# Three edits behind the attention of an encoder layer: which engine forms the differences, when one matrix is split, and how many buffers the embeddings use

## The chip, the cores and the metric

The kernel runs on one core of a Trainium2 chip. Its engines work through queues of their own, each in order: TensorE (PE; its weight loads are listed as PEld), VectorE (DVE), ScalarE (ACT), GpSimd (POOL) and SyncE (SP), which issues the DMAs here. The metric is the device time of one execution in microseconds.

## The reference

One layer of a bidirectional encoder is applied to two sequences of 2048 tokens and width 1024 that share the weights, all in float32. Cut to what matters:

```
proj = rms_norm(x) @ w_in                    # 3328 columns
o_a  = windowed_attention(...) * silu(g_a)   # 8 heads, window +-128
o_b  = neighbourhood_attention(...) * silu(g_b)
x    = x + concat([o_a, o_b]) @ w_out        # 1024 x 1024
gate = sigmoid(x @ w_ple_gate)               # 1024 x 1024
y    = x + (p @ w_ple) * gate                # p: 2048 x 256
```

The change lies in the last three lines: the product with `w_ple` (the embeddings) and the two square products, called the tail here.

## The kernel before

**Precision.** Each matmul of two float32 operands is done as three matmuls of rounded operands. An operand is split: ScalarE writes its rounded copy (hi), VectorE subtracts that from the original (lo), and TensorE adds hi·hi, hi·lo and lo·hi in one PSUM bank. Weights are split by `split_w` (L163 on ACT, L164 on DVE), the tail's activations by `piece` (L1064 on ACT, L1065 on DVE).

**Stream and attention.** Until about 1874 us a generator gives out projection matmuls one by one, and the attention's steps are placed between them at set shares of a unit's cost. `pump` takes one waiting weight split from the list `jobs`; `flush` takes all up to a given one. The last five units of the attention have no projections left, so `ple_ahead(0)` to `ple_ahead(4)` fill them: the embeddings of 512 tokens each, eight output tiles `m` of six matmuls. A result goes from PSUM (`pple`, tag "pj", three banks) by an ACT copy (L870) into a buffer `ev`, and from there by a DMA (L871) into the array `ple_d`. In this part `ev` has two buffers. The tag "sq", also with two buffers of that size, belongs to the projections: the squares and, last, the values `vb` (L692), which a DMA stores (L700).

**Behind the attention** `ple_ahead(5)` to `ple_ahead(7)` run with `tail=True`. They use five buffers of the tag "s". Each output tile also calls `pump` (L865). The list is empty there, but for one case: the last loop is halted after 24 matmuls, the first four operands of the tail are made, and `load_q(0, "s2")` issues four loads of 256 KB and puts their splits on the list. The rest of the loop then takes these four splits between its result copies. The loads for "s1", "s3" and "s4" follow when the loop is done.

**The tail** computes each square product for 1024 tokens by Strassen's scheme (Winograd's form): seven block products in place of eight, at the price of sums of blocks. The sums of weight blocks (s1 to s4) were formed earlier and lie in `sums`. The sums of activation blocks are `combos`: per group 16 subtractions of 128x512 tiles (L1028), four on DVE and twelve on POOL. There are eight groups, four of stage 0 (`w_out`) and four of stage 1 (`w_ple_gate`). A group has seven steps `i`; step `i` runs `product(m, mi)` for four `mi`, 12 matmuls each (L1082). In step `i` the loop calls, for each `mi`: `combos` (in steps 0, 2 and 3), two `piece`s of the next step's operand (for `mi` 0 and 1), then the product and its `result`. In steps 0, 2, 3 and 6 a result starts (stage 0: a DVE sum L1117; stage 1: an ACT copy L1120, in step 6 a tanh from PSUM); in steps 1, 4 and 5 it is finished with a DVE sum (L1126). A finished result of stage 1 goes through tanh on ACT (L1130) and two DVE instructions (L1131, L1132). Eight accumulators share PSUM; the ones of step 1 use the three banks of the tag "sc" for four products, and steps 2, 3 and 6 add to the banks that step 0 began.

**Order.** `P` is `tc.keep_in_program_order`: what it wraps stays in the order of the program on its engine. All of the tail is wrapped, and TensorE's order is fixed throughout. In the splits of the next stage, `load_q(1, ...)` in group 3, four splits are flushed behind each of the steps 3 to 6 of group 3 and 0 to 2 of group 4.

The call that takes the four splits of "s2" if they are still waiting, ahead of step 1 of group 0:

```
if n == 0:
    flush({1: "0s2", 2: "0s1", 3: "0s3", 5: "0s4"}.get(i))
```

Of the kernel before, what the change touches and what calls it, by code (L numbers as in the profile page):

```python
# [11 lines left out]
F32 = mybir.dt.float32  # L12
# [68 lines left out]
TW = 512  # L81
# [17 lines left out]
def emit(ctx, tc, io):  # L99
    nc = tc.nc  # L100
# [4 lines left out]
    def ptile(shape, tag, name):  # L105
        tag = PSM.get(tag, tag)
        return pp.tile(shape, F32, tag=tag, name=name, bufs=PSB[tag])
# [61 lines left out]
    def pump(n=1):  # L169
        for _, job in jobs[:n]:  # L170
            job()
        del jobs[:n]

    def flush(key):
        pump(max((i + 1 for i, (k, _) in enumerate(jobs) if k == key), default=0))
# [35 lines left out]
    def mm(out, lhsT, rhs, start, stop):  # L211
        pinned(nc.tensor.matmul(out, lhsT, rhs, start=start, stop=stop))  # L212
# [61 lines left out]
    ap = ab_stack.enter_context(tc.tile_pool(name="ab", bufs=1))  # L274
# [534 lines left out]
    def load_p(n):  # L809
        if n < len(tiles):  # L810
            s, u = tiles[n]
            p_st[n] = []
            for k in range(2):
                st = main.tile([128, TW], F32, tag="stage", name="p32", bufs=2)
                nc.sync.dma_start(st, io["p_t"][s][128 * k:128 * k + 128, TW * u:TW * u + TW])
                p_st[n].append(st)

    def split_p(n, later=False):

        t = p_rs[n] = main.tile([128, 2, 2, TW], F32R, tag="xr", name="p_r", bufs=2)  # L820

        def job(hi, lo, src):
            nc.scalar.copy(hi, src)
            nc.vector.tensor_tensor(out=lo, in0=src, in1=hi.bitcast(F32), op=ALU.subtract)
        for k, src in enumerate(p_st.pop(n)):
            todo = partial(job, t[:, k, 0], t[:, k, 1], src)
            if later:
                jobs.append((f"p{n}", todo))
            else:
                todo()  # L830
# [19 lines left out]
    def ple_ahead(n, tail=False):  # L850

        load_p(n + 1)
        for m in range(KT):
            ps = ptile([128, TW], "pj", "pple")
            if m == 5 and n + 1 < len(tiles):
                split_p(n + 1)
            flush("p")
            flush("p0")
            for k in range(2):
                w, c = early["p"][2 * (m // 4) + k], 128 * (m % 4)  # L860
                for i, (a, b) in enumerate(((0, 0), (0, 1), (1, 0))):
                    mm(ps, w[:, a, c:c + 128], p_rs[n][:, k, b], k == 0 and i == 0, k == 1 and i == 2)
                    yield 215
            if n > 0 or m > 5:
                pump()  # L865
            if tail:
                ev = main.tile([128, TW], F32, tag="s", name="ev", bufs=SB)
            else:
                ev = ap.tile([128, TW], F32, tag="ev", name="ev", bufs=2)
            P(nc.scalar.copy(ev, ps))  # L870
            nc.sync.dma_start(ple_d[n][:, m], ev)  # L871

# [40 lines left out]
    def paired(f, n):  # L913
# [19 lines left out]
        else:  # L933
            for name in ("a11", "a12", "a22"):
                load_early(name)
        w_b[half] = w

    stream = chain(*(paired(f, last[f]) if f in last else filler(f) for f in range(2, 6 * NT) if f - 1 not in last),
                   *(ple_ahead(n) for n in range(AHEAD)))
    drain(stream, 24)  # L940
    done = 2
# [32 lines left out]
    with tc.tile_pool(name="c", bufs=1, reuse_waits="tile") as op:  # L974
# [44 lines left out]
        def each(fn, k, *blocks):  # L1019

            views = [t[:, k] for t, _ in blocks]
            if any(by_col for _, by_col in blocks):
                views = [v.rearrange("p (c r x) -> p r c x", c=4, x=16) if by_col else
                         v.rearrange("p (r c x) -> p r c x", c=4, x=16) for v, (_, by_col) in zip(views, blocks)]
            P(fn(*views))

        def less(eng, n, k, out, a, b):
            each(lambda x, y, z: eng.tensor_tensor(out=x, in0=y, in1=z, op=ALU.subtract), k,  # L1028
                 *(raws[n, i] for i in (out, a, b)))

        def combos(n, i, k):

            if i == 0:
                if k == 0:
                    raws[n, 4] = op.tile([128, 4, TW], F32, tag="raw", name="raw", bufs=5), False
                less(nc.vector, n, k, 0, 2, 0)
                less(nc.gpsimd, n, k, 4, 3, 0)
            elif i == 2:
                less(nc.gpsimd, n, k, 2, 3, 2)
            elif i == 3:  # L1040
                less(nc.gpsimd, n, k, 4, 1, 4)

        pair = []

# [92 lines left out]

        load_raw(0, 0)
        drain(ple_ahead(AHEAD, True))
        load_raw(0, 1)  # L1140
        drain(ple_ahead(AHEAD + 1, True))
        flush("a22")
        for _ in range(4):
# [13 lines left out]
        for m in range(7 * len(groups)):  # L1157
            n, i = divmod(m, 7)
            if i >= 3:
                load_raw(n + 1, i - 3)  # L1160
            if n == 0:
                flush({1: "0s2", 2: "0s1", 3: "0s3", 5: "0s4"}.get(i))
            for mi in range(4):
                combos(n, i, mi)
                for k in range(2 * mi, 2 * mi + 2) if mi < 2 else ():
                    piece(m + 1, k)
                result(n, i, mi, product(m, mi))
            if n == n_o - 1:
                load_q(1, STEPS[i])
                if i >= 3:  # L1170
                    flush("1" + STEPS[i - 3])
            elif n == n_o and i < 3:
                flush("1" + STEPS[i + 4])
# [76 lines left out]
```

## Time and profile before

| | us |
|---|---|
| median of 3 runs | 2554.75 (2552.64 to 2556.46) |
| the profiled execution, its own time | 2549.44 |
| its span, first to last instruction | 2547.2 |
| TensorE busy | 2486.1 (98%) |
| VectorE busy | 1946.9 (76%) |
| ScalarE busy | 1443.8 (57%) |
| GpSimd busy | 733.2 (29%) |

The profile page is one execution. Its parts used here are the busy times, the chain of work that ended last, the waits (who waited for whom, total us, times, longest), the groups by line (busy, mean ns, idle before), the timeline (start, duration, engine, line, what; in brackets the idle time before it and its releaser) and a table by stretches of time. TensorE's mean granted clock is 0.994 of full speed.

### The profile page before, as it was taken

What the parts mean: (1) busy time and instruction counts of PE and PEld (TensorE: products, weight loads), DVE (VectorE), ACT (ScalarE), POOL (GpSimd) and SP (SyncE); (2) the same over time, 40 slices, a digit from 0 to 9 for tenths busy, and PEclk for the clock granted to TensorE, in tenths of its full rate; (3) what the DMA queues carried; (4) which work ended last, traced back from release to release, by engine and by line L of the source; (5) the groups of instructions that cost most, each with busy time, mean ns of one, the idle gap of its engine ahead of it and who ended that gap; (6) DMA issues with size and microseconds to landing.
All of it is one profiled execution on the core that took longest, in us unless ns stands there. A gap on an engine that the chain in (4) does not pass through costs nothing.

```text
span 2547.2 us, 41396 instructions
## 1 busy us (share of the span) xinstructions
PE 2486.1 (98%) x12912; PEld 2091.2 (82%) x12912; DVE 1946.9 (76%) x5764; ACT 1443.8 (57%) x3469; POOL 733.2 (29%) x969
## 2 busy tenths in 40 slices
PE   8999999999989999999899999999989999999998
PEld 7888888888877888888788888887777888878787
DVE  7888888888887777787877877877635655677876
ACT  6666666666664566666666666666753222344343
POOL 3333323332322333333233332222102221132320
PEclk9999999999999999999999999999999999999999
DMA  5323332111143555555755555456776455746664
GB/s 198 103 97 110 104 97 93 53 59 57 63 112 113 167 185 158 183 182 161 238 164 165 184 176 156 145 156 213 250 253 213 158 166 180 269 159 213 222 231 158
DMA packets 236044, 405.40 MB, mean 159 GB/s; under 512 B 30864, under 2 KB 85264, under 8 KB 230416
## 3 DMA queue, kind: packets, MB, share of 16 engines
q1 hardware_dynamic: 235824, 402.75, 49.5%
q8 instruction: 103, 1.69, 0.3%
q14 instruction: 117, 0.96, 0.1%
HBM read 297.79 MB, written 122.70 MB: 165 GB/s over the span
## 4 chain that ended last, share of the span: by engine, by line
PE 83%; DVE 8%; DMA 3%; ACT 3%; issue 2%; POOL 0%; SPq 0%; ACTq 0%; DVEq 0%; POOLq 0%
PE pqk L212 13%; PE pvg L212 13%; PE acca L1082 11%; PE accc L1082 8%; PE pq L212 6%; PE pg L212 6%; PE scb L212 3%; PE ptb L215 3%; PE pk L212 3%; PE pob L212 3%; PE sc L212 3%; PE po L212 3%; PE pt L215 3%; PE pple L212 2%; DMA ple_d<-ev 1%
## 5 line engine op out<-in xcount | busy, mean ns | idle before, releaser
L243 ACT ACTIVATE s<-s,nm 128x384 f32<-128x384 f32 (+4 forms) x512 | 307.2, 601 | 337.9 <-DVE nm L238 209.8
L212 PE MATMUL pvg<-wb,xr 128*128 128x512 f32 x1536 | 462.1, 408 | 0.0
L212 PE MATMUL pqk<-wa,xr 128*128 128x512 f32 x1536 | 443.9, 411 | 0.0
L308 POOL TENSOR_TENSOR xr<-stx,xr 128x512 fp32r<-128x512 f32 x190 | 244.7, 1295 | 187.3 <-ACT xr L307 181.2
L212 PEld LDWEIGHTS pqk<-wa,xr 128*128 128x128 f32 x1536 | 267.0, 189 | 37.8
L212 PEld LDWEIGHTS pvg<-wb,xr 128*128 128x128 f32 x1536 | 268.4, 190 | 31.6
L1028 POOL TENSOR_TENSOR raw<-raw 128x512 f32<-128x512 f32 x96 | 152.3, 1614 | 460.7 <-DVE raw L1028 284.8
L1064 ACT CAST opd<-raw 128x512 fp32r<-128x512 f32 x224 | 130.4, 620 | 256.6 <-PE acca L1082 105.5
L1065 DVE TENSOR_TENSOR opd<-raw,opd 128x512 fp32r<-128x512 f32 x224 | 183.1, 853 | 120.0 <-ACT opd L1064 120.0
L212 PE MATMUL pg<-wb,xr 128*128 128x512 f32 x768 | 232.1, 410 | 0.0
L212 PE MATMUL pq<-wa,xr 128*128 128x512 f32 x768 | 219.8, 399 | 2.0 <-DVE wa L160 1.6
L798 POOL TENSOR_TENSOR o_tb<-otb 128x256 f32<-128x256 f32 x64 | 47.9, 748 | 549.9 <-DVE otb L791 466.4
L1082 PE MATMUL accc<-opd,wb 128*128 128x512 f32 x768 | 178.6, 392 | 2.8 <-DVE r L1126 2.8
L1082 PE MATMUL acca<-opd,s 128*128 128x512 f32 x768 | 177.5, 390 | 2.8 <-ACT r L1120 2.4
L1082 PE MATMUL acca<-opd,wa 128*128 128x512 f32 x768 | 175.9, 389 | 0.5 <-DVE opd L1065 0.5
L1082 PEld LDWEIGHTS accc<-opd,wb 128*128 128x128 f32 x768 | 145.2, 189 | 33.5 <-DVE r L1126 3.2
L1082 PEld LDWEIGHTS acca<-opd,s 128*128 128x128 f32 x768 | 143.5, 188 | 35.5 <-ACT r L1120 4.0
L1082 PEld LDWEIGHTS acca<-opd,wa 128*128 128x128 f32 x768 | 144.1, 188 | 30.8 <-DVE opd L1065 0.9
L212 PEld LDWEIGHTS pq<-wa,xr 128*128 128x128 f32 x768 | 139.1, 188 | 25.2 <-DVE wa L160 3.0
L212 PEld LDWEIGHTS pob<-p_t,vw 128*128 128x128 f32 (+2 forms) x832 | 132.5, 189 | 31.4 <-DVE p_t L772 7.1
L212 PEld LDWEIGHTS pg<-wb,xr 128*128 128x128 f32 x768 | 138.0, 190 | 20.6
L227 DVE CUSTOM_DVE_ANT_0 s<-scb,bias 128x288 f32<-128x288 f32 (+3 forms) x256 | 141.2, 552 | 16.8 <-PE scb L212 13.8
(171 smaller groups left out, 5330.8 us busy)
## 6 DMA issues: line engine op xcount, KB each, us to landing
stx<-x_b SPq DMA_DIRECT2D x128, 256.0 KB
vw<-v_d SPq DMA_DIRECT2D x112, 256.0 KB
stx<-x_a SPq DMA_DIRECT2D x64, 256.0 KB
stn<-x_n SPq DMA_DIRECT2D x64, 256.0 KB
v_d<-vb SPq DMA_DIRECT2D x64, 256.0 KB
ple_d<-ev SPq DMA_DIRECT2D x64, 256.0 KB
xres<-x_r SPq DMA_DIRECT2D x64, 256.0 KB
x_d<-r SPq DMA_DIRECT2D x64, 256.0 KB
```

The costliest lines, as they stand in the source:

```text
L212: pinned(nc.tensor.matmul(out, lhsT, rhs, start=start, stop=stop))
L215: pinned(nc.tensor.transpose(out, in_, eye))
L227: nc.vector.tensor_tensor_reduce(out=s[:, :n], in0=ps[:, :n], in1=bias, scale=1.0, scalar=-3.0e38, op0=ALU.add, op1=ALU.max, accum_out=sm[ ...
L243: ex = nc.scalar.activation(ss[i][:, :n], ss[i][:, :n], AF.Exp, bias=nm[:, i:i + 1], accum_out=den[:, i:i + 1])
L308: low.tensor_tensor(out=lo, in0=raw, in1=hi.bitcast(F32), op=ALU.subtract)
L798: nc.gpsimd.tensor_tensor(out=o_t, in0=got["ot"][:, :, 0], in1=got["ot"][:, :, 1], op=ALU.add)
L1028: each(lambda x, y, z: eng.tensor_tensor(out=x, in0=y, in1=z, op=ALU.subtract), k, *(raws[n, i] for i in (out, a, b)))
L1064: P(nc.scalar.copy(hi, v))
L1065: P(nc.vector.tensor_tensor(out=lo, in0=v, in1=hi.bitcast(F32), op=ALU.subtract))
L1082: pinned(nc.tensor.matmul(ps, w[k][:, a, c:c + 128], o[:, b], start=i in (0, 1, 4) and k == 0 and j == 0, stop=k == 3 and j == 2, skip_gro ...
```

## The change

Three edits:

- In `combos`, the three kinds of subtraction that ran on GpSimd run on VectorE, at the same places of the program. GpSimd has no work left in the tail.
- `ple_ahead` with `tail=True` no longer calls `pump`. The four splits of "s2" are then taken by the `flush` ahead of step 1 of group 0. The loads keep their place.
- `ple_ahead` without `tail` takes its result buffer from the tags "ev" and "sq" in turn, two tiles each: m 0 and 1 from "ev", 2 and 3 from "sq", and so on, so four buffers in place of two. The tail's loops keep their five.

```diff
-            if n > 0 or m > 5:
+            if not tail and (n > 0 or m > 5):
                 pump()
             if tail:
                 ev = main.tile([128, TW], F32, tag="s", name="ev", bufs=SB)
             else:
-                ev = ap.tile([128, TW], F32, tag="ev", name="ev", bufs=2)
+                ev = ap.tile([128, TW], F32, tag=("ev", "sq")[m // 2 % 2], name="ev", bufs=2)
             P(nc.scalar.copy(ev, ps))
             nc.sync.dma_start(ple_d[n][:, m], ev)
...
                 less(nc.vector, n, k, 0, 2, 0)
-                less(nc.gpsimd, n, k, 4, 3, 0)
+                less(nc.vector, n, k, 4, 3, 0)
             elif i == 2:
-                less(nc.gpsimd, n, k, 2, 3, 2)
+                less(nc.vector, n, k, 2, 3, 2)
             elif i == 3:
-                less(nc.gpsimd, n, k, 4, 1, 4)
+                less(nc.vector, n, k, 4, 1, 4)
```

## The prediction

> **What bounds the kernel now.** I read the page first (busy times, chain), then the table by stretches, then waits and timeline at the three places that the change touches.
>
> ```profile
> span 2547.2 us, 41396 instructions
> PE 83%; DVE 8%; DMA 3%; ACT 3%; issue 2%; POOL 0%; SPq 0%; ACTq 0%; DVEq 0%; POOLq 0%
> core 0: us, PE busy (x) PEld busy (x) DVE busy (x) ACT busy (x) POOL busy (x), PEclk, DMA share, GB/s
> 1903.00:1919.40 16.40, 6.24 (x18) 4.67 (x17) 4.24 (x7) 4.22 (x8) 1.07 (x1) 0.69 0.78 291
> 1919.40:2223.80 304.40, 304.40 (x1344) 252.14 (x1343) 185.48 (x261) 79.54 (x139) 71.57 (x48) 1.00 0.59 196
> 2223.80:2528.20 304.40, 298.33 (x1299) 243.77 (x1299) 226.23 (x299) 123.83 (x228) 79.66 (x48) 0.99 0.59 195
> 1930.31 11.04 PE L1082 MATMUL accc<-opd,wb 128*128 128x512 f32 x48
> 1941.19 1.07 PE L1082 MATMUL acca<-opd,s 128*128 128x512 f32 x4
> 2528.18 11.04 PE L1082 MATMUL acca<-opd,wa 128*128 128x512 f32 x48
> ```
>
> TensorE carries the chain. A step of 48 matmuls takes 1941.19 − 1930.31 = 10.88 us, 0.2267 us each. Stage 0 of the tail keeps TensorE busy for all of its 304.40 us: nothing there can be gained. Time is lost in three places: the stream before 1874 us, a hole at 1904 to 1919, and stage 1, where the 55 steps ahead of the last one should take 55 × 10.88 = 598.4 us and take 2528.18 − 1919.42 = 608.8 (the first row of the tail is quoted with the hole): 10.4 us lost. Each edit touches one of them.
>
> **The change part by part. First, the split in the last embeddings' loop.**
>
> ```profile
> 1874.03 30.21 PE L212 MATMUL pple<-p_r,wa 128*128 128x512 f32 x132
> ...
> 1899.78 1.08 SPq L1016 DMA_DIRECT2D raw<-ob_d  x1
> 1902.62 5.95 SPq L996 DMA_DIRECT2D s<-sums  x4
> 1913.24 0.62 ACT L163 CAST s<-s 128x512 fp32r<-128x512 f32 x1 [10.34 <-DMA s<-sums]
> ...
> 1914.40 5.19 PE L212 MATMUL pple<-p_r,wa 128*128 128x512 f32 x12 [10.16 <-ACT ev L870]
> ...
> 1919.42 11.05 PE L1082 MATMUL acca<-opd,wa 128*128 128x512 f32 x48
> 1908.00:1912.00 4.00, 0.00 (x0) 0.00 (x0) 0.00 (x0) 0.00 (x0) 0.00 (x0) 0.61 1.05 381
> 1912.00:1916.00 4.00, 1.60 (x4) 1.31 (x5) 1.48 (x3) 2.76 (x6) 0.00 (x0) 0.50 0.39 148
> ```
>
> The first split of "s2" waits 10.34 us for its load, which SP issued at 1902.62. Behind it in ScalarE's queue stand the result copies of the last loop; their banks stay full, and TensorE stands still for 10.16 us. When it goes on, its granted clock is 0.50, and the last 12 matmuls take 5.19 us instead of 12 × 0.2267 = 2.72: another 2.5. Without the split in that queue, the three loops' 144 matmuls run through: 1874.03 + 144 × 0.2267 = 1906.7, where the tail now starts at 1919.4. That is **12.7 us**.
>
> The four splits move to step 1 of the tail, four ACT and four DVE instructions of some 0.6 us per queue place (2.4 us). TensorE waits for them only at step 2, 10.88 us later. The loads keep their place; in SP's queue the stores of the last loop and the loads behind them (x, "s1", "s3", "s4") move up by as much as the copies do. The DMA engines ran nearly dry by 1916 (share 0.39), before step 1 begins at 1906.7 + 10.9 = 1917.6. What is late next is an activation block: the sums of step 0 need the two blocks of 1 MB issued up to 1899.78, and the DMA engines are full (share 1.05) until about 1912. If VectorE starts on them at 1912 instead of 1906.7, it has ten instructions of 0.61 us up to the last operand of step 1: 1918, against 1917.6 + 2.0 (nine matmuls into the step). So it still fits, but it uses up the margin, and a stream that arrives some us earlier would meet the same transfers. I take 12.0, with 8 as the other end.
>
> **Second, four result buffers in the stream.** Three rows of the waits between 1770 and 1875 us, two of the timeline, one of the chain, one of SP's timeline:
>
> ```profile
> ACT ev L870 <- DMA ple_d<-ev: 13.3, 12, 2.8
> PE pple L212 <- ACT ev L870: 2.9, 4, 1.7
> PE pob L212 <- DVE p_t L772: 2.6, 4, 0.8
> 1831.79 0.59 ACT L870 COPY ev<-pple 128x512 f32<-128x512 f32 x1 [2.81 <-DMA ple_d<-ev]
> 1832.43 1.65 PE L212 MATMUL pple<-p_r,wa 128*128 128x512 f32 x6 [1.68 <-ACT ev L870]
> 1826.19 5.52 DMA ple_d<-ev
> 1781.85 1.18 SPq L700 DMA_DIRECT2D v_d<-vb  x2
> ```
>
> With two buffers, a copy waits for the store of the copy before the last; a store takes up to 5.5 us. ScalarE loses 13.3 us in 12 waits, but TensorE has other work in most of them: it loses 2.9 us to result copies (the worst, 1.68, is behind a wait of 2.81), and part of the 2.6 us of attention products that need a split queued behind such a copy. Four buffers give a store two more copies' time. I take **3 us**. The bounds: −0.5 at the low end (a copy into "sq" must wait for the store of `vb`, issued at 1781.85 and so possibly not landed at the third copy), 5.5 if both rows go altogether.
>
> **Third, the sums on VectorE.**
>
> ```profile
> L1028 POOL TENSOR_TENSOR raw<-raw 128x512 f32<-128x512 f32 x96 | 152.3, 1614 | 460.7 <-DVE raw L1028 284.8 <-DMA raw<-x_d 172.8 <-DVE opd L1065 3.2
> L1065 DVE TENSOR_TENSOR opd<-raw,opd 128x512 fp32r<-128x512 f32 x108 | 85.9, 835 | 39.6 <-ACT opd L1064 39.6
> L1131 DVE SCALAR_TENSOR_TENSOR r<-r,xres 128x512 f32<-128x512 f32 x64 | 51.9, 810 | 33.5 <-ACT r L1130 33.5
> L1132 DVE SCALAR_TENSOR_TENSOR r<-r,xres 128x512 f32<-128x512 f32 x64 | 50.2, 784 | 2.2
> L1126 DVE TENSOR_TENSOR r<-accc,r 128x512 f32<-128x512 f32 x48 | 32.8, 683 | 1.2 <-PE accc L1082 1.2
> L164 DVE TENSOR_TENSOR s<-s 128x512 fp32r<-128x512 f32 x8 | 9.4, 1230 | 3.7 <-ACT s L163 3.7
> 2227.70 0.69 DVE L1028 TENSOR_TENSOR raw<-raw 128x512 f32<-128x512 f32 x1
> 2228.30 1.28 DVE L1065 TENSOR_TENSOR opd<-raw,opd 128x512 fp32r<-128x512 f32 x2
> ```
>
> These are groups by line, POOL's over the whole tail and VectorE's over stage 1. Alone, a VectorE instruction of this size lasts 0.69 us, and the next follows after 0.60 to 0.61 (2227.70 to 2228.30). While POOL subtracts, the VectorE instructions whose inputs both lie in SBUF (L1065, L1131, L1132, L164) are long, and L1126, which reads PSUM, is not: 683 ns. In stage 1 the lengthening sums to 108 × 0.15 + 64 × 0.12 + 64 × 0.09 + 8 × 0.54 = 34 us. The edit adds 48 subtractions there, 48 × 0.61 = 29.3 us. So VectorE's bill in stage 1 does not grow: 226.2 of 304.4 us busy before, about 220 after, and POOL's 1.6 us per subtraction leaves the way of the operands.
>
> Now the stalls of 10.4 us, one by one:
>
> ```profile
> 2236.29 6.86 DVE L164 TENSOR_TENSOR s<-s 128x512 fp32r<-128x512 f32 x4 [3.70 <-ACT s L163]
> ...
> 2246.08 4.61 PE L1082 MATMUL accc<-opd,wb 128*128 128x512 f32 x12 [2.81 <-DVE r L1126]
> ...
> 2359.17 0.62 ACT L1064 CAST opd<-raw 128x512 fp32r<-128x512 f32 x1 [4.33 <-PE accc L1082]
> ...
> 2385.13 9.38 PE L1082 MATMUL acca<-opd,wa 128*128 128x512 f32 x40 [0.47 <-DVE opd L1065]
> ...
> 2418.33 1.96 PE L1082 MATMUL acca<-opd,s 128*128 128x512 f32 x7 [1.44 <-ACT r L1120]
> ...
> 2532.81 0.68 DVE L1126 TENSOR_TENSOR r<-accc,r 128x512 f32<-128x512 f32 x1
> ...
> 2535.53 0.68 DVE L1126 TENSOR_TENSOR r<-accc,r 128x512 f32<-128x512 f32 x1
> ```
>
> At 2236 the four splits of "s3" take 6.86 us under POOL instead of 2.5; the bank of step 1's first product is read late, TensorE stands for 2.81 us, and its next 12 matmuls take 4.61 us instead of 2.72. Without POOL those splits end at 2238.8 and the bank is read near 2241, before it is wanted. This place gives 2.8 + 1.9 = 4.7 us.
>
> The stall at 2418.33, and smaller ones at the same place of two other groups, come a step and a half after POOL's long run. In step 1 a finished result costs VectorE 2535.53 − 2532.81 = 2.72 us, since it waits for tanh; under POOL, with L1131 and L1132 1 us longer each, it costs 4.7. Four of them and four operands then reach far into step 2, and the copy that frees a bank is behind them. At 2.72 us each, step 1's work is 4 × 2.72 + 4 × 0.61 = 13.3 us, 2.4 more than the step; with what step 0 leaves over it ends 4 to 8 us into step 2, where VectorE has 8 × 0.61 = 4.9 us to do, and the copy comes some 3 us before it is wanted. These stalls go, about 4 us with their restarts.
>
> The stall at 2385.13 (0.5, with its restart 0.8) stays: it follows steps 4 and 5, which have no sums, and starts from an operand that waits for its buffer until the last product of the step (2359.17). And where splits and sums meet, in steps 1 and 2 of group 4, VectorE has 20 and 12 places; I count about 1 us of stall there. Of the 10.4 us, 0.8 + 1.0 are left; I take **8.5 us** as the gain. Ends: 10.4, if none is left, and 0, if VectorE's queue keeps TensorE waiting as often as now. Stage 0 gains nothing, and its queue of 16 places in step 0 (9.8 us of 10.88) is covered.
>
> One rule bears on the 1.9 us of slow matmuls at 2246. The Trainium skill ("TensorE: Matmul & The Clock Gate", section "What's actually happening") says that the clock falls back only after an idle window of about 3.4 us; by that a stall of 2.81 us should cost nothing more. The trace disagrees: the clock in that stretch is below 1.
>
> ```profile
> 2244.00:2248.00 4.00, 1.92 (x6) 1.53 (x7) 3.30 (x4) 1.76 (x3) 3.16 (x3) 0.85 0.00 0
> ```
>
> The row decides; by the page the third part would be 6.6 and the sum 1.9 us smaller.
>
> **The sum.** 12.0 + 3.0 + 8.5 = 23.5 us. The profiled execution took 2549.44 us, 2.2 more than its span, so 2525.9 after. It lies 5.3 us below the median of the runs (2554.75); the same distance added gives **2531 us**.
>
> **Rivals.** *(a) The sums take VectorE's relief.* The removed lengthening and the added places are nearly equal (34 against 29), so the stalls of stage 1 may only change places. For it speaks that a held operand (2359.17) makes VectorE idle and then crowds four more sums behind it; against it, that the worst stalls follow instructions of 1.7 us. Then only 15 us are gained: 2540.
>
> *(b) The hole moves.* TensorE comes 13 to 16 us earlier to data that the same full DMA engines bring (share 1.05). If it waits for the activation blocks or for "s1", half of the 12 us is lost and the clock may fall again: about 2537 to 2541. Against it: the engines were dry by 1916, and three steps have their weights before.
>
> *(c) Slower.* VectorE becomes the bound of stage 1. It decides if an operand's last quarter ends later than 2.0 us into its own step in every group, for instance if the lengthening is not POOL's doing and stays. Then the 48 places of 0.61 us lie on the path: 29.3 − 15 = 14 us slower, 2569. Against it stands L1126 at 683 ns in the same stretches. Beside it stands the Trainium skill ("Perfetto Trace Analysis", section "Optimizing Scalar/DVE Operations"): with VectorE saturated, work should go off it, even to GpSimd. It adds that the two share a port, so that this might not help; VectorE's 226 of 304 us say not saturated.
>
> *(d) It does nothing.* The stalls are re-formed elsewhere by the same amount: 2555. Only the hole's wait speaks on this, and it is removed by construction.
>
> **Chances and range.** The forecast (gain 17 to 29 us) 0.70; (a) 0.13; (b) 0.09; (c) 0.05; (d) 0.03. Range 2523 to 2544: below, all three at their upper ends (12.7 + 5.5 + 10.4 = 28.6, 2526, and 3 us of spread of the medians); above, (a) and (b) with as much spread. A measurement here tells about 0.2%, 5 us, from no change: faster 0.92, same 0.03, slower 0.05.
>
> **What would show it.** Right: no wait of ACT for "s" loads ahead of the tail, and the first tail matmul within 33 us of the last attention product; no or few waits of result copies for stores before 1874; all of VectorE's 128x512 instructions at 0.69 us in the tail, POOL idle; stage 1 losing about 2 us instead of 10.4. Wrong: long VectorE instructions without POOL; operand waits of TensorE at the heads of steps 0 to 3; a clock below 1 at the start of the tail.

## The result

| | before | changed |
|---|---|---|
| median of the runs | 2553.69 us (2551.26 to 2556.46, 4 runs) | 2526.36 us (2525.09 to 2528.4, 4 runs) |
| the profiled execution | 2549.44 us | 2525.68 us |
| its span | 2547.2 us | 2523.8 us |

The ratio of the medians is 0.9893, 95% interval 0.9876 to 0.9911: about 27 us faster.

The changed kernel's profile, in the views that were shown of the kernel before. First the chain that ended last, by engine, and the table by stretches (stretch, its length, busy time and count of PE, PEld, DVE, ACT and POOL, TensorE's clock, DMA share, GB/s) for the start of stage 0 and for all of stage 1, up to its last matmul:

```profile
PE 86%; DVE 6%; DMA 3%; ACT 3%; issue 1%; POOL 0%; SPq 0%; DVEq 0%; ACTq 0%; POOLq 0%
1902.60:2207.20 304.60, 302.72 (x1335) 250.21 (x1335) 193.91 (x312) 81.93 (x142) 0.00 (x0) 1.00 0.62 205
2209.53:2515.34 305.81, 305.21 (x1345) 251.90 (x1343) 229.56 (x360) 128.07 (x233) 0.00 (x0) 1.00 0.61 202
```

All of stage 1 in the kernel before, cut in the same way (the row of the prediction ends 10.6 us ahead of the stage's last matmul):

```profile
2224.07:2538.84 314.77, 308.70 (x1345) 252.38 (x1343) 234.37 (x312) 127.27 (x233) 79.66 (x48) 0.99 0.59 196
```

GpSimd is gone from the tail. In stage 1 VectorE does 48 instructions more (360 against 312), and its busy time is 229.56 us, where it was 234.37. TensorE now stands still for only 0.6 us of stage 1, where it was 6.1, and, which is new, for 1.9 us of stage 0.

The largest groups by line of VectorE from 2209 us to the end, and the three waits of TensorE that are left in the tail:

```profile
L1065 DVE TENSOR_TENSOR opd<-raw,opd 128x512 fp32r<-128x512 f32 x109 | 71.3, 686 | 40.4 <-ACT opd L1064 40.4
L1132 DVE SCALAR_TENSOR_TENSOR r<-r,xres 128x512 f32<-128x512 f32 x64 | 44.3, 692 | 2.2
L1131 DVE SCALAR_TENSOR_TENSOR r<-r,xres 128x512 f32<-128x512 f32 x64 | 44.2, 691 | 33.6 <-ACT r L1130 33.6
L1028 DVE TENSOR_TENSOR raw<-raw 128x512 f32<-128x512 f32 x64 | 42.7, 686 | 2.3 <-DMA raw<-x_d 1.8
L1126 DVE TENSOR_TENSOR r<-accc,r 128x512 f32<-128x512 f32 x48 | 32.8, 684 | 1.1 <-PE accc L1082 1.1
```
```profile
PE accc L1082 <- DVE r L1126: 1.9, 1, 1.9
PE acca L1082 <- DVE opd L1065: 0.6, 2, 0.4
```

Every VectorE instruction of this size has the same duration now, 684 to 692 ns; the means of 784 to 835 are gone.

The place where the hole was, in the timeline of the changed kernel:

```profile
1869.89 32.91 PE L212 MATMUL pple<-p_r,wa 128*128 128x512 f32 x144
1902.65 11.12 PE L1082 MATMUL acca<-opd,wa 128*128 128x512 f32 x48
1913.60 8.32 PE L1082 MATMUL accc<-opd,wb 128*128 128x512 f32 x36
1923.80 1.43 PE L1082 MATMUL accc<-opd,wb 128*128 128x512 f32 x5 [1.88 <-DVE r L1126]
```

The three loops' 144 matmuls run in one piece, and the tail follows at 1902.65. From the last attention product to the tail it was 45.4 us and is 32.8. A stall of 1.88 us stands in step 1 of the first group.

From such timelines the span of every profiled kernel can be cut at the same five matmuls: the first of the embeddings, the last of the attention, the first of the tail, the first of stage 1 and the last of all. "Start" is when the first cut lies; no edit touches what is before it.

| profiled kernel | start | stream | loops | stage 0 | stage 1 | rest |
|---|---|---|---|---|---|---|
| before | 1774.9 | 99.1 | 45.4 | 304.7 | 314.8 | 8.4 |
| changed | 1775.6 | 94.3 | 32.8 | 306.9 | 305.8 | 8.4 |
| third edit alone (sums) | 1777.6 | 99.9 | 46.1 | 305.1 | 305.8 | 9.4 |
| second alone (no splits) | 1776.6 | 100.9 | 35.3 | 312.2 | 314.8 | 8.3 |
| first alone (buffers) | 1778.1 | 94.2 | 44.8 | 304.7 | 313.9 | 9.3 |
| second and third | 1777.3 | 100.9 | 34.0 | 306.4 | 305.8 | 8.5 |
| changed, late loads | 1776.5 | 94.2 | 32.8 | 305.0 | 305.9 | 8.3 |
| changed, GpSimd reads | 1777.7 | 94.3 | 32.8 | 309.5 | 310.3 | 8.6 |
| changed, GpSimd writes | 1775.7 | 94.3 | 32.8 | 306.1 | 305.9 | 8.5 |
| second alone, late loads | 1778.8 | 99.3 | 32.8 | 312.1 | 314.9 | 8.9 |

The change moved the stretches by −4.8, −12.6, +2.2 and −9.0 us: −24.2, and with 0.8 us from the start and the rest, −23.4 of span. (Each stage has 1344 matmuls, 304.7 us at full rate; stage 1 is cut where its last one starts, 304.4.)

### The profile page after: what moved, and what is told of

The parts are those of the page before. It is cut to its first block, busy times and chain, and to the rows that moved or that the text cites. A ratio compares the mean times of both kernels' runs of the same rounds, so it can differ in the third digit from the quotient of the medians.

```text
span 2523.8 us, 41360 instructions
## 1 busy us (share of the span) xinstructions
PE 2478.9 (98%) x12912; PEld 2090.0 (83%) x12912; DVE 1948.5 (77%) x5860; ACT 1445.0 (57%) x3469; POOL 582.5 (23%) x873
## 4 chain that ended last, share of the span: by engine, by line
PE 86%; DVE 6%; DMA 3%; ACT 3%; issue 1%; POOL 0%; SPq 0%; DVEq 0%; ACTq 0%; POOLq 0%
PE pqk L212 13%; PE pvg L212 13%; PE acca L1082 12%; PE accc L1082 9%; PE pq L212 6%; PE pg L212 6%; PE scb L212 3%; PE ptb L215 3%; PE pob L212 3%; PE sc L212 3%; PE pk L212 3%; PE po L212 3%; PE pt L215 3%; PE pple L212 3%; ACT s L243 1%
## 5 line engine op out<-in xcount | busy, mean ns | idle before, releaser
L1065 DVE TENSOR_TENSOR opd<-raw,opd 128x512 fp32r<-128x512 f32 x224 | 146.3, 685 | 111.8 <-ACT opd L1064 111.8
L646 DVE SCALAR_TENSOR_TENSOR ks_b<-pktb,wk,ks_b 64x128 fp32r<-64x128 f32 x256 | 115.1, 450 | 43.9 <-ACT ks_b L645 33.4
```

Source lines behind the costliest of these rows:

```text
L646: nc.vector.scalar_tensor_tensor(out=lo, in0=pkt[a:a + 64, i], scalar=wk[a:a + 64, 1:2], in1=hi.bitcast(F32), op0=ALU.mult, op1=ALU.subtract)
L1065: P(nc.vector.tensor_tensor(out=lo, in0=v, in1=hi.bitcast(F32), op=ALU.subtract))
```

## The experiments

**Each edit alone.** The third:

```diff
-                less(nc.gpsimd, n, k, 4, 3, 0)
+                less(nc.vector, n, k, 4, 3, 0)
...
-                less(nc.gpsimd, n, k, 2, 3, 2)
+                less(nc.vector, n, k, 2, 3, 2)
...
-                less(nc.gpsimd, n, k, 4, 1, 4)
+                less(nc.vector, n, k, 4, 1, 4)
```

> Only the third edit: the 96 sums of GpSimd on VectorE; the splits of the last embeddings' loop and the two result buffers as before. Theory (GpSimd lengthens VectorE's instructions, and that made stage 1's stalls): stage 1 loses about 1.5 us instead of 10.4, the hole of 10 us ahead of the tail stays, time 8 to 9 us below the kernel before. Rival (the sums take the relief): within 2 us of before. Rival (VectorE becomes the bound): slower.

Measured: 2545.68 us against 2553.13, ratio 0.9969 (0.9958 to 0.9981), 7.5 us, a little less than the 8 to 9 expected. Stage 1 takes 305.8 us, as in the changed kernel; the hole is there (a wait of 9.3 us). So the sums cost VectorE nothing that TensorE notices, and the rivals of no gain and of a loss are out.

The second:

```diff
-            if n > 0 or m > 5:
+            if not tail and (n > 0 or m > 5):
                 pump()
```

> Only the second edit: the last embeddings' loop takes no splits; sums stay on GpSimd. Theory: the hole of 12.6 us goes and a stall of about 2 us stands in step 1 of group 0 instead; stage 1 loses its 10.4 us as before; time 10 to 12 us below the kernel before. Rival (the moved splits meet GpSimd's sums and late blocks, and the hole only moves): 6 us or less.

Measured: 2551.56 us against 2553.13, ratio 0.9991 (0.9982 to 0.9999): 1.6 us. Here my theory fell and the rival came true. The timeline of this run, step 1 of group 0, TensorE's and VectorE's rows:

```profile
1928.51 6.46 DVE L164 TENSOR_TENSOR s<-s 128x512 fp32r<-128x512 f32 x4
...
1937.89 2.50 PE L1082 MATMUL accc<-opd,wb 128*128 128x512 f32 x5 [5.91 <-DVE r L1126]
```

and the same four splits in the changed kernel:

```profile
1919.46 2.48 DVE L164 TENSOR_TENSOR s<-s 128x512 fp32r<-128x512 f32 x4
```

The loops lose 10 us, but the moved splits run while GpSimd subtracts, take 6.46 us instead of 2.48, and the bank that the fourth product of step 1 needs is read late: TensorE waits 5.91 us, and its clock falls once more (0.50 from 1934.1 to 1940.9). Stage 0 gives back 7.5 of the 10.1 us. (That the loops take 35.3 us here and 32.8 in the changed kernel is another slow stretch: the clock is 0.51 from 1876 to 1883.)

The first:

```diff
-                ev = ap.tile([128, TW], F32, tag="ev", name="ev", bufs=2)
+                ev = ap.tile([128, TW], F32, tag=("ev", "sq")[m // 2 % 2], name="ev", bufs=2)
```

> Only the first edit: four result buffers in the stream. Theory: the embeddings beside the attention end 4 to 5 us earlier, and as the loads behind them move up too, 4 to 5 us of it reach the end. Rival (the DMA engines are full ahead of the tail): the first split of s2 still lands at the same time, the hole grows by what the stream won, and the time is within 1.5 us of before.

Measured: 2545.65 us against 2553.13, ratio 0.9974 (0.9964 to 0.9983): 4 to 9 us. The stream takes 94.2 us instead of 99.1 (in the table, 94.2 to 94.3 with four buffers and 99.1 to 100.9 with two), and the loops keep their length (44.8): the loads ahead of the hole move up with the stream. The rival, that the full DMA engines eat the gain, is out.

**Second and third together.** The two diffs above, two result buffers in the stream.

> The second and third edits together, the result buffers of the stream as before (two). If the second edit pays only when GpSimd no longer lengthens the splits that it moves into step 1, the two together win about 20 to 22 us, 10 or more beyond the sum of the two alone (7.5 and 1.6); the stream keeps its 99 to 100 us, stage 0 takes 305 to 307. If the edits only add, they win 9 to 10.

Measured: 2534.34 us against 2552.18, ratio 0.9929 (0.9916 to 0.9941): 17.8 us. The two alone give 7.5 and 1.6; together nearly twice their sum. It is some 3 us less than I expected: the stream of this profile took 100.9 us, and 1.2 us more went in the loops. The mechanism is the one of the second run: stage 0 takes 306.4 us here, 312.2 there.

**Is it GpSimd's reading?** The changed kernel, with a subtraction on GpSimd that nobody needs behind each moved sum:

```diff
+        waste = op.tile([128, TW], F32, tag="waste", name="waste", bufs=1)
+        def idle(n, k, out):
+            v = raws[n, out][0][:, k]
+            P(nc.gpsimd.tensor_tensor(out=waste, in0=v, in1=v, op=ALU.subtract))
...
                 less(nc.vector, n, k, 4, 3, 0)
+                idle(n, k, 4)
```

and likewise behind the other two.

> The changed kernel, and GpSimd in addition does one subtraction of the same shape behind each of the 96 moved sums, from the sum's result in SBUF into a tile that nobody reads. Theory (GpSimd's reading of SBUF lengthens VectorE's instructions): L1065, L1131, L1132 and L1028 come back to means of 0.75 to 0.95 us, VectorE's bill is then larger than in either kernel, stage 1 takes 10 us or more beyond its 304.6, and most of what the third edit won is lost: 8 to 25 us above the changed kernel. Rival (it was GpSimd's own 1.6 us on the way of the operands): VectorE's instructions or not, TensorE does not wait, time within 2 us of the changed kernel.

Measured: 2535.18 us against 2553.70, ratio 0.9925 (0.9908 to 0.9942), 8 to 9 us above the changed kernel (0.9893). The groups by line from 2207 us on (L1074, L1140, L1141 and L1135 are L1065, L1131, L1132 and L1126 in the changed kernel), and the stretch of all of stage 1:

```profile
L1074 DVE TENSOR_TENSOR opd<-raw,opd 128x512 fp32r<-128x512 f32 x112 | 98.2, 913 | 14.0 <-ACT opd L1073 14.0
L1028 DVE TENSOR_TENSOR raw<-raw 128x512 f32<-128x512 f32 x64 | 49.7, 795 | 1.6 <-DMA raw<-x_d 1.0
L1141 DVE SCALAR_TENSOR_TENSOR r<-r,xres 128x512 f32<-128x512 f32 x64 | 45.0, 703 | 2.2
L1140 DVE SCALAR_TENSOR_TENSOR r<-r,xres 128x512 f32<-128x512 f32 x64 | 44.8, 700 | 33.8 <-ACT r L1139 33.6
L1135 DVE TENSOR_TENSOR r<-accc,r 128x512 f32<-128x512 f32 x48 | 32.8, 683 | 0.0
2214.34:2524.61 310.27, 307.34 (x1344) 251.15 (x1343) 263.00 (x360) 127.95 (x233) 73.92 (x48) 1.00 0.61 199
```

Work that no result depends on makes VectorE's instructions long again and costs 4.5 us in stage 1 and 2.6 in stage 0. It is less than my 10 us for stage 1. VectorE is busy for 263.0 us of stage 1 here, more than in the kernel before (234.4), and TensorE still loses less than there. What is different is which instructions are long: GpSimd now runs right behind each sum, so the operands' L1074 are hit (913 ns) and the finished results hardly (700 and 703, before 810 and 784), while GpSimd's long run before fell on step 1, where VectorE has the least slack. How much of the rest was that, and how much the operands' wait for GpSimd itself, no run here separates. The chain of the kernel before speaks for the long instructions: ahead of its stall at 2246 it runs through two splits (3.47 us), two operands (2.27 us) and the result's sum (0.61 us) on VectorE, and through no instruction of GpSimd.

The same with memsets, which only write:

```diff
-            v = raws[n, out][0][:, k]
-            P(nc.gpsimd.tensor_tensor(out=waste, in0=v, in1=v, op=ALU.subtract))
+            for _ in range(3):
+                ins = P(nc.gpsimd.memset(waste, 0.0))
+                tc.add_manual_dep(ins.ins, last_less[0].name, ...)   # behind the sum
```

> As the run before, but GpSimd only writes: behind each of the 96 moved sums, three memsets of the waste tile (about 1.6 us), each started by that sum. If reading is what lengthens VectorE's instructions, they stay at 0.69 us and the time is within 2 us of the changed kernel; if any work of GpSimd does it, they are lengthened as in the run before.

Measured: 2527.35 us against 2553.70, ratio 0.9893 (0.9878 to 0.9907), the changed kernel's. Its groups by line, GpSimd's in the tail and VectorE's operands in stage 1:

```profile
L1037 POOL MEMSET waste<- 128x512 f32 x288 | 152.0, 528 | 458.0 <-DVE raw L1030 444.3
L1079 DVE TENSOR_TENSOR opd<-raw,opd 128x512 fp32r<-128x512 f32 x109 | 71.3, 686 | 41.0 <-ACT opd L1078 41.0
```

GpSimd is as busy as in the kernel before (152.0 against 152.3 us), and VectorE's instructions stay at 686 ns. So a GpSimd that reads lengthens VectorE's instructions, and one that is as busy but only writes does not. The Trainium skill says the same ("SBUF — State Buffer", section "Who interferes with whom"): a VectorE instruction with two SBUF inputs contends with a GpSimd instruction that reads SBUF, not with one that only writes.

**The new stall.** The loads of "s2" behind the last loop:

```diff
             piece(0, k)
-        load_q(0, "s2")
         drain(rest)
+        load_q(0, "s2")
```

> The changed kernel, with the four loads of s2 issued behind the last embeddings' loop instead of in its middle (their split stays ahead of step 1). Theory: the stall of 2 us in step 1 of group 0 comes from the stores of the last loop, which stand behind these four loads in the issuing queue for 6.5 us, so that ScalarE waits 7.6 us for a result buffer; with the loads behind the stores that wait is under 2 us and the stall goes: 2 us below the changed kernel, 25 to 29 below the kernel before. Rival (the two activation blocks that VectorE waits for set the stall): the stall stays within 0.5 us. Rival (s2 now lands too late): a wait of ScalarE for s2 ahead of step 1, time equal to the changed kernel or above.

Measured: 2524.32 us against 2553.13, ratio 0.9889 (0.9877 to 0.9902). TensorE's matmuls have no stall left in step 1 of this profile (stage 0 305.0 us). But the wait of ScalarE for a result buffer, which I expected under 2 us, is still 6.68 us, where it was 7.62. Rows of the timeline, VectorE (DVE) and ScalarE (ACT), first of the changed kernel, then of this one, there with TensorE's first matmul of the tail:

```profile
1904.22 0.69 DVE L1028 TENSOR_TENSOR raw<-raw 128x512 f32<-128x512 f32 x1 [4.49 <-DMA raw<-oa_d]
1907.23 0.69 DVE L1028 TENSOR_TENSOR raw<-raw 128x512 f32<-128x512 f32 x1 [2.31 <-DMA raw<-ob_d]
1907.35 1.87 ACT L870 COPY ev<-pple 128x512 f32<-128x512 f32 x3 [7.62 <-DMA ple_d<-ev]
```
```profile
1903.47 11.04 PE L1082 MATMUL acca<-opd,wa 128*128 128x512 f32 x48
1904.08 0.69 DVE L1028 TENSOR_TENSOR raw<-raw 128x512 f32<-128x512 f32 x1 [3.53 <-DMA raw<-oa_d]
1906.91 0.69 DVE L1028 TENSOR_TENSOR raw<-raw 128x512 f32<-128x512 f32 x1 [2.14 <-DMA raw<-ob_d]
1907.24 1.82 ACT L870 COPY ev<-pple 128x512 f32<-128x512 f32 x3 [6.68 <-DMA ple_d<-ev]
```

Counted from the tail's first matmul, the second activation block is there after 4.6 us in the changed kernel and after 3.4 us here, and ScalarE's held copies start after 4.7 and 3.8 us: with "s2" out of the way both come about 1 us earlier. Which of the two sets the stall this run does not separate. The rows speak for the copies: ScalarE is through with them at 1909.2 and 1909.1, later than VectorE with the sum of the second block (1907.9 and 1907.6), and the operands of step 1 stand behind them in ScalarE's queue. To see whether this beats the changed kernel, both ran once more side by side:

> The changed kernel once more, beside the next run on the same chip: 2525 to 2528, a stall of 1 to 2 us in step 1 of group 0.

> The changed kernel with the late loads of s2 once more, to see whether it beats the changed kernel: 1 to 2 us below it if the stall in step 1 of group 0 is all that differs, and no stall there.

Measured: 2527.14 and 2526.98 us, ratios 0.9899 (0.9886 to 0.9913) and 0.9896 (0.9881 to 0.9911). They cannot be told apart; the stall is 1.7 us in the one and 0.9 us in the other. No version here is shown to beat the changed kernel.

Last, the late loads with the second edit alone, where GpSimd still subtracts:

> Only the second edit (sums on GpSimd, two buffers in the stream), with the four loads of s2 issued behind the last embeddings' loop. The second edit alone had a stall of 6 us in step 1 of group 0. If the stores held behind those loads set that stall, it goes: 8 us or more below the second edit alone. If GpSimd, under which the four moved splits took 6.5 us, sets it, 3 us or more of it stay.

Measured: 2548.81 us against 2553.70, ratio 0.9982 (0.9972 to 0.9992). The stall is 4.7 us, stage 0 takes 312.1 us (312.2 without the late loads), and the four splits take 6.50 us. So the large stall is GpSimd's: without its subtractions the same edit left 1.47 us of stall (second and third together). The blocks, stores and loads make only the last 2 us.

## Why the prediction was right

The forecast of 2531 us is 4.6 above the median, and inside its range. By its own sum it came closer: 23.5 us off the profiled execution gave 2525.9, and the profiled execution took 2525.68. That it came so close is luck: the three terms missed by −1.6, +1.8 and +0.5 us, and 0.8 us went in parts that no edit touches. What failed is the last step, "the same distance added": the profiled execution of the kernel before lay 4 to 5 us below its median, that of the changed kernel 0.7. The start column shows part of why: what no edit touches took 1774.9 us there and 1775.6 to 1778.8 in the other profiles of the table, so that execution was an early one, and a distance of one execution from its median is not a property of the kernel.

By terms:

- **The split in the last loop, 12.0.** The loops gave 12.6 us, as summed (12.7: 10.2 of wait and 2.5 of slow clock). The doubt named beside it came true: VectorE waits for the two blocks (4.49 and 2.31 us) under full DMA engines (share 0.96 to 1.05 from 1898 to 1926), and 2.2 us are lost in stage 0. TensorE meets it at another place, not at an operand but at the fourth product of step 1: its bank is read by a sum (L1126) that stands in VectorE's queue behind the four moved splits (2.48 us). The prediction asked only when TensorE wants these splits, at step 2, and not what waits behind them. The net is 10.4, between the value taken and the end of 8. What I overlooked there is ScalarE: its last result copies wait for stores on the same full engines (7.62 us), ahead of the operands of step 1.
- **Four buffers, 3.** Measured 4.8, between the value and the bound of 5.5. The waits were counted rightly: TensorE's idle time in the stream fell from 8.1 to 5.1 us, by 3.0. What the sum left out is that the same 495 matmuls kept TensorE busy for 89.1 us instead of 90.9, with the clock at 1.00 in both. The restart behind each wait (13 waits before, 9 now), which the third term counted and this one did not, may be part of that; no run here shows where the 1.8 us went. The wait for the store of `vb` did not appear.
- **The sums, 8.5.** Stage 1 gave 9.0. The bill of VectorE came out as added up, 34 us less and 29 more: it fell by 4.8 us. The 226 and 220 us of the prediction are too small for the whole stage, since its row leaves out the last 10 us; they were 234.4 and 229.6. The stall at 2385 stayed as foretold (0.45 us and its restart, now at 2364.89), and where splits and sums meet in group 4 TensorE loses some 0.6 us instead of the 1 us counted: it waits 0.15 us for an operand at 2244.47, eight matmuls into step 3. That is one of the waits named as a sign of being wrong, in small.
- **The rule on the clock.** The runs do not settle at which gap the clock falls, see below; the stall of 2.81 us is gone with its slow matmuls, as the row had it.

Of the rivals, (a) and (c) fell with the third edit alone. (b) holds for 2.2 us. What the prediction did not see is how the second and third edits depend on each other: it priced the moved splits at 2.4 us, which is right only because the sums had left GpSimd. Added one by one they would have given 9 us, not 18.

## What to carry to other kernels

Ahead of moving work off a waiting queue, ask who runs beside the place where it goes: four splits cost 2.5 us there with GpSimd idle, 6.5 with GpSimd reading, and that decided whether 10 us were won or 2. An engine that adds 96 instructions can be hardly busier for it (VectorE 1948.5 us over the whole kernel, where it was 1946.9), if the engine that did them before slowed it down; compare means of one instruction with and without the neighbour. And test edits alone and in pairs: three that gave 7.5, 1.6 and 7.5 us gave 27 together.

## What was not expected of the hardware

TensorE's clock after short waits. At the end of the attention stand three waits of TensorE of 0.4, 0.8 and 0.8 us within 4.1 us, in every profile (its weight loads wait 0.6, 1.0 and 1.0 us there). In the kernel before, the clock behind them is 1.00; with the third edit alone it is 0.58 in the same place. The tables by stretches, of the kernel before and of that run:

```profile
1874.00:1880.00 6.00, 6.00 (x29) 4.98 (x28) 1.12 (x3) 2.55 (x5) 0.74 (x1) 1.00 0.54 180
```
```profile
1876.00:1880.00 4.00, 3.42 (x11) 2.94 (x12) 2.16 (x5) 0.83 (x2) 0.74 (x1) 0.58 0.39 135
```

and a stall of 1.88 us in the changed kernel left the clock at 1.00:

```profile
1920.00:1924.00 4.00, 2.12 (x10) 1.46 (x9) 4.00 (x8) 0.00 (x0) 0.00 (x0) 1.00 1.03 334
```

So in these runs the clock could fall after waits of at most 0.8 us and could stay after one of 1.9, and the same waits had different outcomes in different executions. A slow stretch also outlasts its cause: after the stall that ended at 2246.08 in the kernel before, the clock is 1.00 up to 2246.7, 0.50 from 2246.8 to 2250.1 and 1.00 from 2250.2; with the third edit alone it is 0.50 from 1876.64 to 1880.05. What decides whether it falls stays open: in the 3.41 us just ahead of these two stretches TensorE was busy for 0.69 and 1.80 us, and in the 3.42 us around the stall of 1.88 us, with no fall, for 1.57 us. The Trainium skill ("TensorE: Matmul & The Clock Gate", section "What's actually happening") has windows of about 3.4 us that run free of the kernel; the varying outcome agrees with that, but a fall without an idle stretch of that length does not.
